# Gates of the PEER experts: high and low halves in one moving operand, one matmul per token

## The chip, the core and the metric

The kernel runs on one core of a Trainium2 chip. TensorE (PE, with its weight loads PEld) multiplies into PSUM banks of 512 float32 values on each of 128 partitions; VectorE (DVE) and ScalarE (ACT) work on SBUF and PSUM; SyncE (SP) issues the transfers. Each engine takes its own instructions in order. The metric is the time on the device in microseconds, median of several runs.

## The reference, cut to what matters

Two transformer blocks on 256 tokens of width 1024. The second has two layers, and each ends in a PEER stage: 16384 experts, of which every token uses 8 heads x 16.

```
def _peer(x, w_q, sub_keys, u, v):
    ...
    expert = idx_a * PEER_N_KEYS + idx_b          # first key a, second key b, 128 each
    gate = jax.nn.softmax(best_s, axis=-1)
    ...
        h = jnp.einsum('td,thkd->thk', xb, u[eb])
        a = (jax.nn.gelu(h, approximate=False) * gb).astype(xb.dtype)
        return jnp.einsum('thk,thkd->td', a, v[eb])
```

The kernel gathers nothing. It computes the hidden value of every expert for every token, multiplies it by a gate that is zero for experts not chosen, and multiplies the result by all of v.

## The kernel before

All matmuls with float32 data run as three passes over a high and a low part (`split`, L224: ScalarE writes `hi`, L225, VectorE writes `lo`, L226). In `peer`, `u_pair(j)` (L1225) loads two second keys' expert weights, splits them (four instructions of 128x1024), runs 48 matmuls of 256 columns (L264 to L266) and writes gelu into the ring `H` (L1228), which holds 80 second keys (`RING`) of 128 first keys by 256 tokens. `v_pair(j)` (L1271) splits two second keys of `H` (`ah`, `al`) and their weights and runs 24 matmuls of 512 columns (L281 to L283).

Between them stand the gates. The second keys are cut in parts of 48, 48 and 32 (`PARTS`), the tokens in groups of 16; so a layer has 48 calls of `gates(part, t0)` (L1230), and the kernel 96. One call does this. VectorE writes the one-hot rows `oa` (first key of each of a token's 128 choices, for 16 tokens) and `ob` (second key), then `oh` and `ol`, which are `ob` times the high and the low half of the gate (L1239 to L1242). The tokens lie innermost, four by four, so that the columns of one token stand 4 half-floats (8 bytes) apart. For each token TensorE multiplies `oa` by `oh` and by `ol` into the same columns of a PSUM bank (L1249, L1250); so the bank holds the sum. Banks of the tag `ms` are taken by eight tokens of 48 columns or sixteen of 32; there are two such banks. VectorE multiplies a full bank into `H` (L1257), in two instructions where the part wraps around the ring (the second part).

The loop at L1318 to L1335 emits the calls: the first part's 16 groups go with `u_pair` 24 to 39, which fills the ring; then u and v alternate; the second part's 16 groups go with u and v in turn, the third part's with v. A planner orders the instructions of each engine by their place in the program and by when their operands are ready in its own account, so matmuls of `u_pair` or `v_pair` can stand between those of one call. Preparation of weights runs 350 instructions ahead (`AHEAD`). `v_pair(0)` waits for all groups of the first part.

Of the kernel before, what the change touches and what calls it, by code (L numbers as in the profile page):

```python
# [9 lines left out]
F32 = mybir.dt.float32  # L10
F32R = mybir.dt.float32r
F16 = mybir.dt.float16
U32 = mybir.dt.uint32
AF = mybir.ActivationFunctionType
ALU = mybir.AluOpType
# [11 lines left out]
ALPHA = 4.0 ** 0.25  # L27
G_SCALE = 2048.0

PARTS = (48, 48, 32)  # second keys of the experts that are gated together  # L30
RING = 80  # second keys whose hidden values are on chip at a time
RATE = 0.96  # groups of 16 tokens gated for each tile of expert weights
AHEAD = 350  # instructions by which the weights' preparation runs ahead
WBUFS = 4  # split halves of weight tiles on chip
LEAD = 2  # tiles of the first block left when its attention is through
PACE = 2  # tiles of expert weights to a step of the selection
TURN = 17  # the tile after which the first half's indices are transposed
# memory keys and values of a layer, computed where norms leave the tensor engine free
FILL = ((), ("k1",), ("v1",), (), ("k0", "v0"))
URGENT = 1500  # instructions by which norms go before other work  # L40


def _btiles(w, cols):
# [128 lines left out]
class Net:  # L172
# [157 lines left out]
    def col(self, name="col", n=1, bufs=None):  # L330
        return self.sp.tile([128, n], F32, name=name, tag=f"{name}{n}")

    def table(self, func):
        """Has the table of func loaded behind the scalar engine's work so far."""
        t = self.col("warm")
        self.tc.keep_in_program_order(self.nc.scalar.activation(t, self.eps6, func))

# [56 lines left out]
    def layer_norm(self, acc, gb, xT=None, out=None):  # L394
# [3 lines left out]
        for tt in range(2):  # L398
# [14 lines left out]
            for nh in range(2):  # L413
# [6 lines left out]
                    nc.sync.dma_start(out[tt * 128:tt * 128 + 128, c], x[:, c])  # L420
                if xT is not None:
                    self.to_T(xT, x[:, c], tt, nk=4, k0=4 * nh)
# [1 line left out]
    def load_mem(self):  # L424
        self.memT = tuple(self.mp.tile([128, 8, S], F32R, name=f"memT{s}") for s in "hl")
        raw = self.raw(self.io["memT"].rearrange("p k t -> p (k t)")).rearrange("p (k t) -> p k t", k=8)
# [392 lines left out]
    def ple_gate(self, acc, bv, xT):  # L819
        nc = self.nc  # L820
        for tt in range(2):
            h = self.vp.tile([128, D], F32, name="hn", tag="hn")
            for nh in range(2):
# [3 lines left out]
                nc.vector.tensor_mul(h[:, c], h[:, c], self.pproj[:, tt, c])  # L827
                nc.vector.tensor_add(self.x[:, tt, c], self.x[:, tt, c], h[:, c])
                self.to_T(xT, self.x[:, tt, c], tt, nk=4, k0=4 * nh)
# [1 line left out]
    def mem_attn(self, qm, km, vm):  # L831
        nc, pp = self.nc, self.pp
        mP = {}
# [266 lines left out]
    def peer(self, l, xT):  # L1100
        nc, io, pp = self.nc, self.io, self.pp
# [5 lines left out]
        idx = [pp.tile([128, S], F16, name=f"pidx{j}") for j in range(4)]  # L1107
        H = pp.tile([128, RING, S], F32, name="H")
        tk = ExitStack()
# [120 lines left out]
        def gates(part, t0):  # L1230
            b0, nb = sum(PARTS[:part]), PARTS[part]
            oa = op.tile([128, 4, P_KEYS, 4], F16, name="oa", tag="oa", bufs=2)
            ob, oh, ol = (op.tile([128, 4, max(PARTS), 4], F16, name=n, tag=n, bufs=k)[:, :, :nb]
                          for n, k in (("ob", 1), ("oh", 2), ("ol", 2)))
            c = slice(t0, t0 + 16)
            col = lambda j, n: idx[j][:, c].rearrange("p (g t) -> p g t", t=4)[:, :, None, :].to_broadcast(
                [128, 4, n, 4])
            iot = lambda n0, n: iota[:, None, n0:n0 + n, :].to_broadcast([128, 4, n, 4])
            nc.vector.tensor_tensor(out=oa, in0=iot(0, P_KEYS), in1=col(0, P_KEYS), op=ALU.is_equal)  # L1239
            nc.vector.tensor_tensor(out=ob, in0=iot(b0, nb), in1=col(1, nb), op=ALU.is_equal)  # L1240
            nc.vector.tensor_tensor(out=oh, in0=ob, in1=col(2, nb), op=ALU.mult)
            nc.vector.tensor_tensor(out=ol, in0=ob, in1=col(3, nb), op=ALU.mult)  # L1242
            nt = 16 if nb <= 32 else 8
            for e in range(16 // nt):
                ps = self.ms()
                for n in range(nt):
                    t = e * nt + n
                    o = ps[:, n * nb:n * nb + nb]
                    nc.tensor.matmul(o, oa[:, t // 4, :, t % 4], oh[:, t // 4, :, t % 4], start=True, stop=False)  # L1249
                    nc.tensor.matmul(o, oa[:, t // 4, :, t % 4], ol[:, t // 4, :, t % 4], start=False, stop=True)  # L1250
                g = ps[:, :nt * nb].rearrange("p (t b) -> p b t", t=nt)
                done = 0
                while done < nb:
                    s = (b0 + done) % RING
                    n = min(nb - done, RING - s)
                    h = H[:, s:s + n, t0 + e * nt:t0 + e * nt + nt]
                    nc.vector.scalar_tensor_tensor(h, g[:, done:done + n], 1.0 / G_SCALE, h, op0=ALU.mult,  # L1257
                                                   op1=ALU.mult)
                    done += n

        acc = {}

# [36 lines left out]
        for tt in range(2):  # L1299
            todo += [lambda tt=tt: pick(tt, 0, 4), lambda tt=tt: pick(tt, 4, 4), lambda tt=tt: gate(tt),  # L1300
                     lambda tt=tt: lookup(tt)]
        n0 = PARTS[0] // 2
        for j in range(n0):
# [10 lines left out]
        op = ok.enter_context(self.tc.tile_pool(reuse_waits="tile", name="onehot", bufs=1))  # L1314
        ends = [sum(PARTS[:k + 1]) // 2 for k in range(len(PARTS))]
        queue = [(k, t0) for k in range(len(PARTS)) for t0 in range(0, S, 16)]
        up, vp, due, turn_v = n0, 0, 0.0, True
# [98 lines left out]
```

## Time and profile before

| what | value |
|---|---|
| median of 3 runs | 2532.6 us (2531.86 to 2533.39) |
| span of the profiled execution | 2531.2 us |
| PE / DVE / ACT busy in that span | 2497.7 / 1733.8 / 1194.2 us |
| gate matmuls (L1249, L1250) | 3072 |
| share of the chain that ended last, PE | 94% |

A "busy" TensorE has at least one matmul in flight; matmuls overlap, so what one costs is read from the distance of their starts. The page's chain of waits names for each stretch of time the engine that the end hung on.

### The profile page before, as it was taken

The page shows a single profiled execution, that of the slowest core. Times are in us where ns is not written, and L with a number is a line of the kernel's source. Part 1 is how long each engine was busy: PE and PEld are TensorE (multiplying, and loading weights), DVE is VectorE, ACT ScalarE, POOL GpSimd, SP SyncE. Part 2 cuts the span into 40 slices and gives each one's busy share as a digit, 9 for nine tenths or more (in the row PEclk, how much of TensorE's full clock was granted, in tenths as well). Part 3 has the DMA queues.
Part 4 walks back from the last instruction along what each step waited for, and adds up shares of the span by engine and source line. Part 5 has one row for each costly group of instructions (what it writes and reads, how often), then busy time and mean ns, then how long its engine had stood idle before and what let it go on. Part 6 is the DMA issues. An engine that isn't in the chain of part 4 may idle for free.

```text
span 2531.2 us, 44590 instructions
## 1 busy us (share of the span) xinstructions
PE 2497.7 (99%) x18560; PEld 2276.9 (90%) x18560; DVE 1733.8 (68%) x3195; ACT 1194.2 (47%) x1697; POOL 5.9 (0%) x17
## 2 busy tenths in 40 slices
PE   8999999999999999999999999999999999999998
PEld 7998899988799999999988888989999999998887
DVE  5357665565699587588478556669968758748756
ACT  5357554455545533433443445644643443344443
POOL 0000000000000000000000000000000000000000
PEclk9989999999999999999999999999999999999999
DMA  8422455543444544544544554344553454454454
GB/s 295 150 96 92 140 209 190 183 173 109 154 170 167 195 142 148 191 157 143 191 167 156 194 195 158 140 175 165 183 179 139 161 189 143 158 183 167 166 187 147
DMA packets 64410, 420.80 MB, mean 166 GB/s; under 512 B 7520, under 2 KB 10480, under 8 KB 15824
## 3 DMA queue, kind: packets, MB, share of 16 engines
q1 hardware_dynamic: 64208, 417.96, 47.4%
q8 instruction: 145, 2.38, 0.4%
q14 instruction: 57, 0.47, 0.1%
HBM read 416.88 MB, written 1.05 MB: 165 GB/s over the span
## 4 chain that ended last, share of the span: by engine, by line
PE 94%; DVE 3%; ACT 1%; DMA 1%; issue 1%; SPq 0%; DVEq 0%; ACTq 0%
PE ps_st L264 15%; PE ps_st L266 15%; PE ps_st L265 15%; PE ps_acc L281 12%; PE ps_acc L283 12%; PE ps_acc L282 12%; PE ps_ms L1249 3%; PE ps_ms L1250 3%; PE ps_sc L621 1%; PE ps_acc L640 1%; DVE lo L226 1%; ACT hi L225 1%; PE ps_acc L1152 1%; PE ps_sc L494 1%; PE ps_ms L1053 0%
## 5 line engine op out<-in xcount | busy, mean ns | idle before, releaser
L226 DVE TENSOR_TENSOR lo<-raw,hi 128x1024 fp32r<-128x1024 f32 (+1 forms) x762 | 922.8, 1214 | 508.5 <-ACT hi L225 505.5
L225 ACT CAST hi<-raw 128x1024 fp32r<-128x1024 f32 (+1 forms) x762 | 792.8, 1043 | 939.7 <-PE ps_st L265 610.1
L264 PE MATMUL ps_st<-xTh,hi 128*128 128x256 f32 (+1 forms) x3232 | 924.0, 286 | 0.9 <-DVE shift_v L573 0.7
L266 PE MATMUL ps_st<-xTh,lo 128*128 128x256 f32 (+1 forms) x3232 | 919.0, 284 | 0.5 <-DVE lo L226 0.5
L265 PE MATMUL ps_st<-xTl,hi 128*128 128x256 f32 (+1 forms) x3232 | 918.3, 284 | 0.0
L264 PEld LDWEIGHTS ps_st<-xTh,hi 128*128 128x128 f32 (+1 forms) x3232 | 619.3, 192 | 5.6 <-issue 2.0
L265 PEld LDWEIGHTS ps_st<-xTl,hi 128*128 128x128 f32 (+1 forms) x3232 | 618.8, 191 | 4.2 <-issue 1.4
L266 PEld LDWEIGHTS ps_st<-xTh,lo 128*128 128x128 f32 (+1 forms) x3232 | 618.4, 191 | 4.5 <-issue 2.7
L281 PE MATMUL ps_acc<-hi,ah 128*128 128x512 f32 x1024 | 403.8, 394 | 0.0
L282 PE MATMUL ps_acc<-lo,ah 128*128 128x512 f32 x1024 | 399.0, 390 | 0.0
L283 PE MATMUL ps_acc<-hi,al 128*128 128x512 f32 x1024 | 398.2, 390 | 0.0
L283 PEld LDWEIGHTS ps_acc<-hi,al 128*128 128x128 f32 x1024 | 192.1, 188 | 40.9
L281 PEld LDWEIGHTS ps_acc<-hi,ah 128*128 128x128 f32 x1024 | 192.9, 188 | 37.5
L282 PEld LDWEIGHTS ps_acc<-lo,ah 128*128 128x128 f32 x1024 | 192.6, 188 | 37.4
L225 ACT CAST ah<-H 128x512 fp32r<-128x512 f32 x128 | 79.5, 623 | 178.4 <-PE ps_acc L282 178.4
L226 DVE TENSOR_TENSOR al<-H,ah 128x512 fp32r<-128x512 f32 x128 | 88.4, 692 | 86.3 <-ACT ah L225 86.3
L1249 PE MATMUL ps_ms<-oh,oa 128*128 128x48 f16 (+1 forms) x1536 | 144.3, 214 | 0.0
L1249 PEld LDWEIGHTS <-oa 128*128 128x128 f16 x1536 | 131.1, 117 | 14.0 <-DVE lo L226 10.5
L1250 PE MATMUL ps_ms<-ol,oa 128*128 128x48 f16 (+1 forms) x1536 | 143.0, 214 | 0.0
L1250 PEld LDWEIGHTS <-oa 128*128 128x128 f16 x1536 | 133.9, 118 | 0.0
L1257 DVE SCALAR_TENSOR_TENSOR H<-ps_ms,H 128x256 f32<-128x256 f32 (+2 forms) x224 | 96.6, 457 | 40.7 <-PE ps_ms L1250 40.5
L1239 DVE TENSOR_TENSOR oa<-iota,pidx 128x2048 f16<-128x2048 f16 x96 | 116.7, 1215 | 0.0
(365 smaller groups left out, 2234.5 us busy)
## 6 DMA issues: line engine op xcount, KB each, us to landing
raw<-in_u SPq DMA_DIRECT2D x128, 1024.0 KB, 4.8
raw<-in_v SPq DMA_DIRECT2D x128, 1024.0 KB, 4.8
raw<-in_w_gu SPq DMA_DIRECT2D x22, 1024.0 KB, 4.8
raw<-in_w_pq SPq DMA_DIRECT2D x16, 1024.0 KB, 4.9
raw<-in_w_out SPq DMA_DIRECT2D x12, 1024.0 KB, 4.9
raw<-in_w_down SPq DMA_DIRECT2D x11, 1024.0 KB, 4.8
raw<-in_b_q SPq DMA_DIRECT2D x9, 1024.0 KB, 4.8
raw<-in_a_vr SPq DMA_DIRECT2D x6, 1024.0 KB, 4.9
```

Of the source, the lines that this page charges most:

```text
L225: self.nc.scalar.copy(hi, src)
L226: self.nc.vector.tensor_sub(lo, src, hi.bitcast(F32))
L264: mm(ps, wh, xh, start=first, stop=False)
L265: mm(ps, wh, xl, start=False, stop=False)
L266: mm(ps, wl, xh, start=False, stop=last)
L281: mm(ps, xh, w[0][:, c], start=first, stop=False)
L282: mm(ps, xh, w[1][:, c], start=False, stop=False)
L283: mm(ps, xl, w[0][:, c], start=False, stop=last)
L1239: nc.vector.tensor_tensor(out=oa, in0=iot(0, P_KEYS), in1=col(0, P_KEYS), op=ALU.is_equal)
L1249: nc.tensor.matmul(o, oa[:, t // 4, :, t % 4], oh[:, t // 4, :, t % 4], start=True, stop=False)
L1250: nc.tensor.matmul(o, oa[:, t // 4, :, t % 4], ol[:, t // 4, :, t % 4], start=False, stop=True)
L1257: nc.vector.scalar_tensor_tensor(h, g[:, done:done + n], 1.0 / G_SCALE, h, op0=ALU.mult, op1=ALU.mult)
```

## The change

`oh` and `ol` become one tile `og` that holds, for each four tokens, the columns of the high half and behind them those of the low half. One matmul per token and part multiplies `oa` by both, so 96 or 64 columns where two matmuls of 48 or 32 wrote into one place. High and low results lie side by side in PSUM, so a bank holds four tokens of 96 columns or eight of 64, half as many as before. ScalarE copies the high columns of a bank to an SBUF tile `gt`, VectorE adds the low ones, and when all 16 tokens are there VectorE multiplies `gt` into `H`. `gt` and `ob` have one buffer, `oa` and `og` two. The lines that only lose a comment are left out here.

```
-            ob, oh, ol = (op.tile([128, 4, max(PARTS), 4], F16, name=n, tag=n, bufs=k)[:, :, :nb]
-                          for n, k in (("ob", 1), ("oh", 2), ("ol", 2)))
+            ob = op.tile([128, 4, max(PARTS), 4], F16, name="ob", tag="ob")[:, :, :nb]
+            og = op.tile([128, 4 * 2 * max(PARTS) * 4], F16, name="og", tag="og", bufs=2)[:, :32 * nb].rearrange(
+                "p (g s b t) -> p g s b t", g=4, s=2, t=4)
+            gt = op.tile([128, max(PARTS) * 16], F32, name="gt", tag="gt")[:, :nb * 16].rearrange(
+                "p (b t) -> p b t", t=16)
...
-            nc.vector.tensor_tensor(out=oh, in0=ob, in1=col(2, nb), op=ALU.mult)
-            nc.vector.tensor_tensor(out=ol, in0=ob, in1=col(3, nb), op=ALU.mult)
-            nt = 16 if nb <= 32 else 8
+            for j in range(2):
+                nc.vector.tensor_tensor(out=og[:, :, j], in0=ob, in1=col(2 + j, nb), op=ALU.mult)
+            nt = 8 if nb <= 32 else 4
             for e in range(16 // nt):
                 ps = self.ms()
                 for n in range(nt):
                     t = e * nt + n
-                    o = ps[:, n * nb:n * nb + nb]
-                    nc.tensor.matmul(o, oa[:, t // 4, :, t % 4], oh[:, t // 4, :, t % 4], start=True, stop=False)
-                    nc.tensor.matmul(o, oa[:, t // 4, :, t % 4], ol[:, t // 4, :, t % 4], start=False, stop=True)
-                g = ps[:, :nt * nb].rearrange("p (t b) -> p b t", t=nt)
-                done = 0
-                while done < nb:
-                    s = (b0 + done) % RING
-                    n = min(nb - done, RING - s)
-                    h = H[:, s:s + n, t0 + e * nt:t0 + e * nt + nt]
-                    nc.vector.scalar_tensor_tensor(h, g[:, done:done + n], 1.0 / G_SCALE, h, op0=ALU.mult,
-                                                   op1=ALU.mult)
-                    done += n
+                    nc.tensor.matmul(ps[:, n * 2 * nb:(n + 1) * 2 * nb], oa[:, t // 4, :, t % 4],
+                                     og[:, t // 4, :, :, t % 4].rearrange("p s b -> p (s b)"), start=True, stop=True)
+                g = ps[:, :nt * 2 * nb].rearrange("p (t s b) -> p s b t", t=nt, s=2)
+                gs = gt[:, :, e * nt:e * nt + nt]
+                nc.scalar.copy(gs, g[:, 0])
+                nc.vector.tensor_tensor(out=gs, in0=gs, in1=g[:, 1], op=ALU.add)
+            done = 0
+            while done < nb:
+                s = (b0 + done) % RING
+                n = min(nb - done, RING - s)
+                h = H[:, s:s + n, t0:t0 + 16]
+                nc.vector.scalar_tensor_tensor(h, gt[:, done:done + n], 1.0 / G_SCALE, h, op0=ALU.mult, op1=ALU.mult)
+                done += n
```

## Rows read from the trace of the kernel before

**Rows 1.** Head of the page: span, and busy time of each engine.
```profile
span 2531.2 us, 44590 instructions
...
PE 2497.7 (99%) x18560; PEld 2276.9 (90%) x18560; DVE 1733.8 (68%) x3195; ACT 1194.2 (47%) x1697; POOL 5.9 (0%) x17
```

**Rows 2.** Busy time by stretch, layer 0: part one, part two, between, part three.
```profile
core 0: us, PE busy (x) PEld busy (x) DVE busy (x) ACT busy (x) POOL busy (x), PEclk, DMA share, GB/s
885.62:988.40 102.78, 102.78 (x1122) 102.21 (x1120) 82.86 (x112) 36.39 (x42) 0.00 (x0) 1.00 0.43 149
1096.12:1197.00 100.88, 100.88 (x954) 92.63 (x953) 88.77 (x148) 36.69 (x42) 0.00 (x0) 1.00 0.45 152
1197.00:1286.80 89.80, 89.80 (x578) 82.10 (x577) 45.11 (x41) 41.73 (x48) 0.00 (x0) 1.00 0.53 182
1300.00:1386.60 86.60, 86.60 (x730) 71.48 (x730) 73.55 (x99) 34.23 (x40) 0.00 (x0) 1.00 0.47 164
```

**Rows 3.** Groups by line and form: matmuls of the high half.
```profile
L1249 PE MATMUL ps_ms<-oh,oa 128*128 128x48 f16 x1024 | 105.8, 226 | 0.0
...
L1249 PE MATMUL ps_ms<-oh,oa 128*128 128x32 f16 x512 | 38.5, 191 | 0.0
```

**Rows 4.** Timeline of PE (start, duration), a group of part one.
```profile
885.38 0.28 PE L265 MATMUL ps_st<-xTl,hi 128*128 128x256 f32 x1
885.50 0.28 PE L266 MATMUL ps_st<-xTh,lo 128*128 128x256 f32 x1
885.62 0.21 PE L1249 MATMUL ps_ms<-oh,oa 128*128 128x48 f16 x1
...
887.14 0.36 PE L264 MATMUL ps_st<-xTh,hi 128*128 128x256 f32 x1
887.34 0.28 PE L265 MATMUL ps_st<-xTl,hi 128*128 128x256 f32 x1
```

**Rows 5.** Timeline of PE, a group of part three.
```profile
1299.99 0.20 PE L1249 MATMUL ps_ms<-oh,oa 128*128 128x32 f16 x1
...
1301.08 0.47 PE L281 MATMUL ps_acc<-hi,ah 128*128 128x512 f32 x1
1301.39 0.39 PE L282 MATMUL ps_acc<-lo,ah 128*128 128x512 f32 x1
1301.62 0.40 PE L283 MATMUL ps_acc<-hi,al 128*128 128x512 f32 x1
```

**Rows 6.** Timeline of DVE, within one step of part one.
```profile
908.62 0.56 DVE L1257 SCALAR_TENSOR_TENSOR H<-ps_ms,H 128x384 f32<-128x384 f32 x1 [0.98 <-PE ps_ms L1250]
909.10 1.22 DVE L226 TENSOR_TENSOR lo<-raw,hi 128x1024 fp32r<-128x1024 f32 x1
```

**Rows 7.** Busy time of one step in parts one, two (two groups) and three.
```profile
892.97:900.31 7.34, 7.34 (x83) 7.30 (x81) 5.92 (x8) 2.59 (x3) 0.00 (x0) 1.00 0.42 145
1124.97:1139.38 14.41, 14.41 (x139) 13.23 (x137) 12.82 (x21) 5.25 (x6) 0.00 (x0) 1.00 0.43 143
1320.00:1326.60 6.60, 6.60 (x57) 5.46 (x56) 5.79 (x9) 2.58 (x4) 0.00 (x0) 1.00 0.44 156
```

**Rows 8.** Groups by line and form: prices of VectorE.
```profile
L1257 DVE SCALAR_TENSOR_TENSOR H<-ps_ms,H 128x384 f32<-128x384 f32 x64 | 35.3, 554 | 30.8 <-PE ps_ms L1250 30.6
...
L1257 DVE SCALAR_TENSOR_TENSOR H<-ps_ms,H 128x256 f32<-128x256 f32 x64 | 26.8, 419 | 9.9 <-PE ps_ms L1250 9.9
...
L1257 DVE SCALAR_TENSOR_TENSOR H<-ps_ms,H 128x512 f32<-128x512 f32 x32 | 21.9, 691 | 0.0
...
L226 DVE TENSOR_TENSOR lo<-raw,hi 128x768 fp32r<-128x768 f32 x16 | 14.9, 949 | 5.7 <-ACT hi L225 5.7
...
L655 DVE TENSOR_TENSOR os<-ps_acc,wsw 128x384 f32<-128x384 f32 x16 | 8.9, 557 | 16.6 <-PE ps_acc L644 16.6
```

**Rows 9.** Groups by line and form: copies of ScalarE out of PSUM.
```profile
L637 ACT COPY PT<-ps_pt 128x512 f32<-128x512 f32 x16 | 9.1, 584 | 2.5 <-PE ps_pt L634 2.5
...
L637 ACT COPY PT<-ps_pt 128x256 f32<-128x256 f32 x16 | 6.0, 372 | 4.3 <-PE ps_pt L634 4.2
```

## The prediction, made blind

> **What bounds the kernel now.** I read the head of the page first: TensorE is busy for 2497.7 of 2531.2 us, VectorE for 68%, ScalarE for 47% [rows 1]. [...] Then the matmuls themselves, by the distance of their starts in the timeline, and the prices of the added work.
>
> **TensorE, gate matmuls.** There are 1024 pairs of 48 columns and 512 of 32 [rows 3], each with as many matmuls of the low half as of the high. A group of 16 tokens issues 32 matmuls. With 48 columns it runs from 885.62 to 887.14: 1.52 us, 47.5 ns a matmul. Behind it the first 256-column matmul takes 0.20 us to the next start, where 0.12 is usual: 0.08 us for leaving the gates [rows 4]. So 1.60 us a group. With 32 columns it is 1299.99 to 1301.08, 34 ns a matmul, and the 512-column matmul behind takes 0.31 instead of 0.23: 1.09 + 0.08 = 1.17 us [rows 5].
>
> What does a matmul of 96 or 64 columns cost? No row shows it with this operand, whose columns lie 8 bytes apart. From 32 to 48 columns the price rises by 13.5 ns, 0.84 ns a column, and 34 = 32 x 0.84 + 7. On that line a matmul of 64 costs 61 ns and one of 96 costs 88; the pair costs 68 and 95. So joining two saves just the 7 ns that do not depend on columns. The other end is the slope of packed operands: from 256 to 512 columns 0.12 to 0.23 us, 0.43 ns a column [rows 4, 5], which gives 47.5 + 48 x 0.43 = 68 and 34 + 32 x 0.43 = 48 ns. I take the first end, since its slope is from this very operand and 47.5 ns for 48 columns is more than twice what 0.43 allows.
>
> [...]
>
> **Bursts.** A group's 16 tokens now need four fillings of the two `ms` banks in parts one and two, where two were enough. The third filling waits until ScalarE has copied and VectorE has added the first. The planner will put u or v matmuls there, and each return to them costs up to the 0.08 us above, or less: the last gate matmul is now longer by 41 ns and can hide that much of the next weights' arrival, so 0.04 to 0.08. With one burst a group costs 16 x 88 ns + 0.04 = 1.45 us; with four at 0.08 it costs 1.73. I take two bursts at 0.06: 1.53 us, 0.07 less than now. 64 groups: 4.5 us gained (bounds: 9.6 gained, 8.3 lost). Part three fits its two banks: 16 x 61 + 80 ns = 1.06 us, 0.11 less; 32 groups: 3.5 us gained. TensorE in all: 8 us gained.
>
> **VectorE.** A step is bounded by starts, and an instruction blocks the next for about 0.08 us less than its duration (0.56 long, next start 0.48 later) [rows 6]. A plain two-operand instruction costs what the fused one costs (557 and 554 for 384 values) [rows 8], so an add of 192 values, on the line through 256 and 384 (1.05 ns a value), takes 0.35 us, or 0.27 blocked. `og` costs what `oh` and `ol` cost: same values, same instructions.
> - Part one, a step of 7.34 us with 5.92 busy [rows 7]: less two of 554 (0.95 blocked), plus four adds (1.08) and one multiply of 768 values (949, so 0.87): 6.92.
> - Part two, two groups in 14.41 us with 12.82 busy [rows 7]: each group loses two of 256 and two of 128 values (419 and, on the same line, 284 ns: 1.09 blocked), gains four adds (1.08), one of 512 (0.61) and one of 256 (0.34): 12.82 + 1.9 = 14.7. That is more than the step. The backlog, 0.3 us x 8 steps, can run into the next stretch, where VectorE is half idle and nothing needs the second part yet.
> - Part three, 6.60 us with 5.79 busy [rows 7]: two adds of 256 (0.34 each) more: 6.47.
>
> So no step is over, or its excess has a place to go, but the reserve falls from 1.4 us to 0.4 in part one and to nothing in the others, and VectorE's in-order queue now waits for ScalarE four times a group. Bounds of these waits: nothing (today TensorE does not stop in any of these stretches with VectorE at 88% [rows 2]), or today's idle time kept on top in part one: 6.92 + 1.42 = 8.34 us for a step of 7.27, 1.07 x 32 steps = 34 us. I take 4 us, nearer to nothing, because that idle time is mostly time in which VectorE has nothing due (0.98 us ahead of one L1257 [rows 6]).
>
> **ScalarE** gets four copies of 192 values (line through 256 and 512, 0.83 ns a value: 0.32 us) or two of 256 (0.37) [rows 9]: 1.3 us on 2.59 of 7.34 busy [rows 7]. That is hidden; its price shows only as the bank's later return. Loads, queues and SP's work are untouched.
>
> **Sum.** 2531.2 - 8 + 4 = 2527.2 us of span; the runs' median stands 1.4 us above the span, so 2528.6; I say 2529.
>
> **Rivals.**
> 1. The columns cost the packed slope: 68 and 48 ns. A group costs 16 x 68 + 2 x 0.06 = 1.21 (0.39 less, 64 times: 25 us) and 16 x 48 + 80 ns = 0.85 (0.32 less, 32 times: 10 us). VectorE then limits part one (6.92 of 6.95) and part two, so some 10 us stay behind: 2532.6 - 25 = 2507. For it: the first gate matmul of a burst lasts as long with 32 columns as with 48 (0.20 and 0.21) [rows 4, 5]. Against it: the steady slope. Chance 0.14.
> 2. VectorE becomes the bound. Place: the 32 steps of part one, whose last group `v_pair(0)` waits for. Price: the 34 us above, of which the planner hides perhaps a third: 2529 + 22 = 2551. It decides once VectorE's waits in a step exceed 7.27 - 6.92 = 0.35 us. For it: four hand-overs from ScalarE where none was, behind casts that themselves wait for TensorE. Against: preparation runs ahead by 350 instructions. Chance 0.17.
> 3. TensorE stops for the bank: the third filling's turn comes before the first is added. A turn is a matmul (0.22), a copy (0.32) and an add (0.35), 0.9 us, of which the second filling covers 0.35; 0.5 us x 64 groups = 32, less the 8: 2556 if the planner puts nothing between, 2540 if it covers two thirds. It decides when ScalarE's cast of 128x1024 stands ahead of a copy. Chance 0.13.
> 4. TensorE's best: one burst, no waits, 2532.6 - 13 = 2519 to 2527. Chance 0.19.
>
> **How the numbers follow.** The forecast, 2529 with its own range 2527.5 to 2537.7, has 0.37, and with the bursts and waits uncertain it is no change that can be told: a measurement of this kernel can tell about 0.2%, 5 us. Faster by more: rivals 1 and 4, 0.33. Slower: 2 and 3, 0.30. The range goes from rival 1 to rival 2, 2506 to 2552, and leaves out a third rival without cover and a first rival without give-back, under 2 in 10.
>
> **What would show it.** Starts of gate matmuls 88 and 61 ns apart: the column price; 68 and 48: rival 1. Runs of 8 gate matmuls split by L264 to L266: the bursts. Idle PE ahead of gate matmuls, ended by the add: rival 3; idle PE ahead of L264 or L281, ended by `lo`, `ah` or `al`: rival 2. VectorE's busy share in part one should be 94 to 97%. The forecast is wrong if the slope per column changes beyond 48, or if TensorE shows idle time in the stretches that have none now.

## The result, and the profile after

The changed kernel takes 2553.5 us (median of 4 runs, 2551.4 to 2556.1) where the kernel before takes 2532.4 in the same session: a ratio of 1.0084, 95% interval 1.0070 to 1.0097. It is slower by 21 us; my range ended at 2552. The profiled execution has a span of 2553.4 us, 22.2 more than before [rows 1].

The head of its page:

```profile
span 2553.4 us, 42136 instructions
...
PE 2499.9 (98%) x17024; PEld 2265.0 (89%) x17024; DVE 1814.2 (71%) x3419; ACT 1275.3 (50%) x2017; POOL 5.9 (0%) x17
```

TensorE's busy time is 2.2 us more than before, so most of what was lost is time in which it has nothing in flight. Busy time by stretch says where (columns as in [rows 2]): layer 0, the steps of part one, their end, and two stretches behind that.

```profile
885.00:990.00 105.00, 105.00 (x923) 103.06 (x922) 92.91 (x145) 51.45 (x99) 0.00 (x0) 1.00 0.43 148
993.10:1005.90 12.80, 4.47 (x42) 3.54 (x41) 12.25 (x23) 4.13 (x11) 0.00 (x0) 0.65 0.23 83
1005.90:1010.60 4.70, 4.70 (x11) 3.73 (x12) 4.21 (x9) 1.50 (x4) 0.00 (x0) 0.50 0.01 3
1012.00:1016.00 4.00, 4.00 (x20) 3.28 (x19) 2.62 (x3) 1.78 (x3) 0.00 (x0) 1.00 0.00 0
```

In the steps TensorE never stops, and VectorE is busy for 88% of them. Then comes a stretch of 12.8 us in which TensorE works for 4.5 and VectorE for 12.3. Inside it the granted clock falls to 0.50, where it stays behind it for a while: 11 matmuls take 4.7 us, where behind that 20 take 4.0. TensorE's timeline of that end (start, duration, idle time before and what ended it):

```profile
992.86 0.28 PE L266 MATMUL ps_st<-xTh,lo 128*128 128x256 f32 x1
996.30 0.89 PE L1251 MATMUL ps_ms<-og,oa 128*128 128x96 f16 x8 [3.17 <-DVE og L1245]
997.75 0.89 PE L1251 MATMUL ps_ms<-og,oa 128*128 128x96 f16 x8 [0.56 <-DVE gt L1256]
999.07 0.89 PE L1251 MATMUL ps_ms<-og,oa 128*128 128x96 f16 x8 [0.43 <-DVE gt L1256]
1002.23 0.88 PE L1251 MATMUL ps_ms<-og,oa 128*128 128x96 f16 x8 [2.28 <-DVE gt L1256]
1004.38 0.89 PE L1251 MATMUL ps_ms<-og,oa 128*128 128x96 f16 x8 [1.27 <-DVE og L1245]
1005.90 0.79 PE L281 MATMUL ps_acc<-hi,ah 128*128 128x512 f32 x1 [0.63 <-ACT ah L225]
```

The last u matmul ahead of the stop starts at 992.86. It belongs to `u_pair(40)`, which the planner has pulled ahead of `v_pair(0)`: the gelu of `u_pair(39)` starts at 986.80. `v_pair(0)` may start when the first part's last group is in `H`, and 40 gate matmuls, two and a half groups, are still to come, with nothing to lay between them. Each eight wait for `og` or for the add that gives a bank back, and `v_pair(0)` for its cast `ah`: 8.3 us idle. Layer 1 has the same rows from 2007 on.

Work of more than two groups is left when the cover ends, although in the steps VectorE stands idle for 12.1 of 105 us, most of it behind ScalarE in the order of its queue (waits of VectorE, 885 to 990: us in total, times, longest):

```profile
DVE gt L1256 <- ACT gt L1255: 5.0, 10, 1.0
DVE lo L226 <- ACT hi L225: 4.0, 6, 1.7
DVE oa L1242 <- PE ps_ms L1251: 1.9, 3, 0.8
```

What is left it does in the stretch behind, where it is busy for 12.3 us and TensorE waits. A second, smaller stop stands in part three:

```profile
1392.58 1.77 PE L283 MATMUL ps_acc<-hi,al 128*128 128x512 f32 x4 [1.52 <-DVE al L226]
```

The gate matmuls, two returns to u matmuls, and the prices of the added work (groups by line and form):

```profile
892.52 0.89 PE L1251 MATMUL ps_ms<-og,oa 128*128 128x96 f16 x8
893.19 0.36 PE L264 MATMUL ps_st<-xTh,hi 128*128 128x256 f32 x1
893.39 0.28 PE L265 MATMUL ps_st<-xTl,hi 128*128 128x256 f32 x1
...
895.90 0.53 PE L1251 MATMUL ps_ms<-og,oa 128*128 128x96 f16 x4
896.20 0.36 PE L265 MATMUL ps_st<-xTl,hi 128*128 128x256 f32 x1
896.41 0.52 PE L1251 MATMUL ps_ms<-og,oa 128*128 128x96 f16 x4
```
```profile
L1256 DVE TENSOR_TENSOR gt<-gt,ps_ms 128x192 f32<-128x192 f32 x256 | 81.3, 350 | 13.3 <-ACT gt L1255 12.8
...
L1255 ACT COPY gt<-ps_ms 128x192 f32<-128x192 f32 x256 | 72.2, 319 | 67.7 <-PE ps_ms L1251 37.4 <-DVE H L1262 24.0 <-DVE ob L1243 5.5
...
L1262 DVE SCALAR_TENSOR_TENSOR H<-gt,H 128x768 f32<-128x768 f32 x32 | 30.5, 954 | 0.0
```

By the distance of their starts (median over all of a form) a matmul of 96 columns costs 90 ns and one of 64 costs 62. A group has mostly three bursts, of 8, 4 and 4. In the rows eight matmuls lead to the next start after 0.67 us, 0.05 under 8 x 90, and that next matmul takes 0.20 instead of 0.12; over all 160 returns from 96 columns to a u matmul the median of this sum is 0.04 us a burst, not 0.08.

**The balance.** Idle time: 8.3 + 1.5 us a layer, 19.7. The profile counts idle time only from the end of the matmul before, so each of the 14 stops takes 0.16 to 0.18 us more from the distance of starts: 2.5. Half clock: v matmuls that start at granted 0.50 stand further apart than at 1.00 (0.43 instead of 0.23 us), together by 2.3 and 1.45 us in layer 0 and 2.0 and 1.5 in layer 1, 7.3; the gate matmuls there keep their 90 ns. That is 29.4; the span grew by 22.2, so matmuls and bursts gave 7.2.

### The profile page after: what moved, and what is told of

Read it like the earlier page. It is cut to its first block, busy times and chain, and to the rows that moved or that the text cites. A ratio compares the mean times of both kernels' runs of the same rounds, so it can differ in the third digit from the quotient of the medians.

```text
span 2553.4 us, 42136 instructions
## 1 busy us (share of the span) xinstructions
PE 2499.9 (98%) x17024; PEld 2265.0 (89%) x17024; DVE 1814.2 (71%) x3419; ACT 1275.3 (50%) x2017; POOL 5.9 (0%) x17
## 4 chain that ended last, share of the span: by engine, by line
PE 92%; DVE 4%; ACT 2%; DMA 1%; issue 1%; SPq 0%; DVEq 0%; ACTq 0%
PE ps_st L264 15%; PE ps_st L265 15%; PE ps_st L266 15%; PE ps_acc L281 12%; PE ps_acc L283 12%; PE ps_acc L282 11%; PE ps_ms L1251 5%; DVE lo L226 1%; PE ps_sc L621 1%; PE ps_acc L640 1%; ACT hi L225 1%; PE ps_acc L1152 1%; PE ps_sc L494 1%; PE ps_ms L1053 0%; PE ps_pt L634 0%
## 5 line engine op out<-in xcount | busy, mean ns | idle before, releaser
L226 DVE TENSOR_TENSOR lo<-raw,hi 128x1024 fp32r<-128x1024 f32 (+1 forms) x762 | 924.0, 1215 | 475.8 <-ACT hi L225 472.3
L282 PE MATMUL ps_acc<-lo,ah 128*128 128x512 f32 x1024 | 405.0, 395 | 0.0
L283 PE MATMUL ps_acc<-hi,al 128*128 128x512 f32 x1024 | 400.8, 394 | 3.0 <-DVE al L226 3.0
L283 PEld LDWEIGHTS ps_acc<-hi,al 128*128 128x128 f32 x1024 | 194.0, 190 | 43.4 <-DVE al L226 4.1
L1251 PE MATMUL ps_ms<-og,oa 128*128 128x96 f16 (+1 forms) x1536 | 163.6, 258 | 15.5 <-DVE og L1245 8.9
L1251 PEld LDWEIGHTS <-oa 128*128 128x128 f16 x1536 | 109.9, 119 | 41.6 <-issue 17.1
L1255 ACT COPY gt<-ps_ms 128x192 f32<-128x192 f32 (+1 forms) x320 | 93.7, 330 | 72.1 <-PE ps_ms L1251 40.1
L1256 DVE TENSOR_TENSOR gt<-gt,ps_ms 128x192 f32<-128x192 f32 (+1 forms) x320 | 105.4, 363 | 13.6 <-ACT gt L1255 12.8
L281 PE MATMUL ps_acc<-hi,xTh 128*128 128x512 f32 (+1 forms) x272 | 108.3, 398 | 5.2 <-ACT xTh L225 3.3
```

The costliest lines, as they stand in the source:

```text
L226: self.nc.vector.tensor_sub(lo, src, hi.bitcast(F32))
L281: mm(ps, xh, w[0][:, c], start=first, stop=False)
L282: mm(ps, xh, w[1][:, c], start=False, stop=False)
L283: mm(ps, xl, w[0][:, c], start=False, stop=last)
L1251: nc.tensor.matmul(ps[:, n * 2 * nb:(n + 1) * 2 * nb], oa[:, t // 4, :, t % 4], og[:, t // 4, :, :, t % 4].rearrange("p s b -> p (s b)"), ...
L1255: nc.scalar.copy(gs, g[:, 0])
```

## The experiments

Times are medians; the kernel before had 2531.9 to 2533.1 in these sessions. A ratio is to it, with its 95% interval.

### Is it the wait for a bank? (e1)

On the changed kernel, every second filling of part one goes to the `acc` banks, which `v_pair` does not hold yet:

```
-                ps = self.ms()
+                ps = self.acc() if part == 0 and e % 2 else self.ms()
```

> The changed kernel, in which every second filling of a group of the first part takes one of the four acc banks that v_pair has not yet claimed, so that a group's four fillings have four banks. Theory A (VectorE's added work of about 1 us a group makes it fall behind in the first part; what is left at its end is worked off with TensorE idle, and the idle time costs the clock): still some 8 us idle a layer behind u_pair 39, 2550 to 2556 us. Theory B (the way fill, copy, add, bank free is too slow for two banks): with four banks the idle time falls under 3 us a layer, 2522 to 2535 us.

Measured: 2562.9 us, 1.0117 (1.0088 to 1.0146), above the range of either theory. Idle time at the end of part one is 6.9 us a layer, most of what it was, now ended by `og` (4.1) and `ah` (2.8) and no more by a bank, and a new stop of 4.4 us stands ahead of an L283 at 1215, ended by `al`. More banks don't cure it, so the return of a bank is where TensorE happens to stand, not why it is late.

### Matmuls alone, hand-over alone, load alone (e3 to e7, e11)

e3 has the joined matmuls but no copies and adds: VectorE multiplies the high half straight into `H` and leaves the low half out.

```
-                nc.scalar.copy(gs, g[:, 0])
-                nc.vector.tensor_tensor(out=gs, in0=gs, in1=g[:, 1], op=ALU.add)
...
+                    h = H[:, s:s + n, t0 + e * nt:t0 + e * nt + nt]
+                    nc.vector.scalar_tensor_tensor(h, g[:, 0, done:done + n], 1.0 / G_SCALE, h, op0=ALU.mult,
+                                                   op1=ALU.mult)
```

> The changed kernel without its sum: VectorE multiplies the high half straight from PSUM into H, four instructions of 192 values a group; the low half is computed and not used, ScalarE's copies and VectorE's adds are left out. It holds the matmuls of the change alone. Theories A and B: no idle time at the end of the first part, and the whole gain of TensorE shows, 7 us a layer: 2514 to 2522 us. If it stays above 2528, the matmuls themselves do not gain.

Measured: 2525.5 us, 0.9964 (0.9948 to 0.9980), no idle TensorE in any gate stretch; the time is above the 2514 to 2522 expected, which counted the gain once for each layer. The head of its page:

```profile
span 2524.0 us, 41718 instructions
...
PE 2489.4 (99%) x17024; PEld 2257.5 (89%) x17024; DVE 1749.9 (69%) x3419; ACT 1193.6 (47%) x1697; POOL 5.9 (0%) x17
```

So joining gives 7 us where VectorE's work is not in the way (span 7.2 under the kernel before), as the balance says (7.2), with all its bursts.

e4 keeps the old pairs and lets ScalarE copy each bank and VectorE multiply once a group. e5 keeps the old pairs and gives each group an add on VectorE that nobody needs (896 values, in part three 576). e7 has both. The first line is e4's, the others are e5's (e7 writes its add as half-floats, which takes as long: 1084 and 1083 ns):

```
+                nc.scalar.copy(gt[:, :, e * nt:e * nt + nt], g)
...
+            scr = op.tile([128, 896], F32, name="scr", tag="scr")[:, :w]
+            nc.vector.tensor_add(scr, self.x[:, 0, :w], self.x[:, 1, :w])
```

> The kernel before, with its pairs of matmuls, but each full bank is copied to SBUF by ScalarE and VectorE multiplies the 16 tokens from there: hand-over to ScalarE without more work for VectorE (one multiply of 768 in place of two of 384). Theory A: as the kernel before, 2529 to 2536 us, no idle TensorE behind u_pair 39. Theory B: idle time of 4 to 8 us a layer there, 2542 to 2555 us.

> The kernel before with one more VectorE instruction a group that nobody waits for: an add of 896 values (576 in the third part), about 1.0 and 0.7 us, the work that the change adds to VectorE, without hand-overs. Theory A: VectorE falls behind, TensorE is idle for 4 to 9 us a layer behind u_pair 39 and loses clock, 2545 to 2562 us. Theory B: as the kernel before, 2529 to 2536 us.

> The kernel before with ScalarE's copy of each full bank to SBUF, one multiply by VectorE from there, and one more VectorE add a group that nobody waits for (896 values, 576 in the third part): load and hand-over together on the old pairs of matmuls, whose step is 7.34 us. Theory A (the shorter step is needed too): 2529 to 2537 us, no idle TensorE behind u_pair 39. Theory B (load and hand-over together make the lag): idle time of 4 to 9 us a layer there, 2542 to 2558 us.

Measured: 2532.8, 1.0004 (0.9993 to 1.0015); 2532.2, 0.9999 (0.9987 to 1.0010); 2532.1, 1.0006 (0.9994 to 1.0017). None has idle TensorE in a gate stretch. e7's stretch of part one:

```profile
885.00:990.00 105.00, 105.00 (x1159) 104.36 (x1158) 98.63 (x116) 47.86 (x72) 0.00 (x0) 1.00 0.43 147
```

VectorE is busier there (94%) than in the changed kernel (88%), and it costs nothing. So VectorE's share doesn't decide.

e6 is e3 with the idle add (768 or 512 values): joined matmuls, load, no hand-over. e11 is the changed kernel with `oa` computed once a part instead of once a group (the other groups' first keys are left out): joined matmuls, hand-over, less load. The first line is e6's, the others are e11's:

```
+            nc.vector.tensor_add(scr, self.x[:, 0, :w], self.x[:, 1, :w])
...
-            nc.vector.tensor_tensor(out=oa, in0=iot(0, P_KEYS), in1=col(0, P_KEYS), op=ALU.is_equal)
+            if t0 == 0:
+                nc.vector.tensor_tensor(out=oa, in0=iot(0, P_KEYS), in1=col(0, P_KEYS), op=ALU.is_equal)
```

> The kernel of the high half alone (matmuls of the change, four multiplies of 192 straight from PSUM, neither copies nor adds; the low half is not used), with one more VectorE instruction a group that nobody waits for, an add of 768 values (512 in the third part): VectorE's load of the change on TensorE's steps of the change, without ScalarE in between. Theory A (load against the shorter step: VectorE's need of 6.9 us plus its usual waits no longer fits a step of 7.1 us): idle TensorE of 4 to 9 us a layer behind u_pair 39, 2535 to 2555 us. Theory B (the load hurts only where it stands in the way from a filled bank to a free one, by way of ScalarE): as without the extra add, 2521 to 2529 us.

> The changed kernel with oa computed only for the first 16 tokens of each part and used for all its groups, so that gates of the other tokens stand at wrong first keys: it takes 1.13 us a group from VectorE and leaves copies, adds, banks and matmuls as they are. Theory A (VectorE's load against TensorE's shorter step): no idle TensorE behind u_pair 39 and no lost clock, 2514 to 2524 us. Theory B (the chain from bank to bank by way of ScalarE): still some 8 us idle a layer, 2545 to 2556 us.

Measured: e6 2540.2, 1.0030 (1.0019 to 1.0042), theory A's; e11 2538.7, 1.0030 (1.0019 to 1.0041), between its two theories. Both stop at the end of part one; TensorE's timelines there, e6 and then e11:

```profile
996.86 0.89 PE L1252 MATMUL ps_ms<-og,oa 128*128 128x96 f16 x8 [1.01 <-DVE og L1243]
999.26 0.88 PE L1252 MATMUL ps_ms<-og,oa 128*128 128x96 f16 x8 [1.51 <-DVE H L1260]
1001.84 0.79 PE L281 MATMUL ps_acc<-hi,ah 128*128 128x512 f32 x1 [1.70 <-ACT ah L225]
```
```profile
994.58 0.89 PE L1256 MATMUL ps_ms<-og,oa 128*128 128x96 f16 x8 [2.54 <-DVE gt L1261]
995.91 0.52 PE L1256 MATMUL ps_ms<-og,oa 128*128 128x96 f16 x4 [0.44 <-DVE gt L1261]
996.64 0.52 PE L1256 MATMUL ps_ms<-og,oa 128*128 128x96 f16 x4 [0.21 <-DVE gt L1261]
998.63 0.79 PE L281 MATMUL ps_acc<-hi,ah 128*128 128x512 f32 x1 [1.47 <-ACT ah L225]
```

On the joined matmuls the two causes add up, as far as medians of runs that spread over 3 to 6 us can tell: neither (e3) 2525.5, load 14.7 more, hand-over 13.2 more, both (the changed kernel) 28.0 more. In e11 VectorE is busy for 84.5 of the 105 us (before: 83.6), so there the chain from matmul to copy, add and multiply makes the stop by itself.

### How late the groups are

The stop is read best from one distance: the end of a group's last multiply behind the start of the gelu of the u pair it was emitted with, group 1 with `u_pair(24)` to group 16 with `u_pair(39)`. Four rows give the last group's, the first two of the kernel before, the others of the changed one (timelines of ACT and DVE):

```profile
989.47 0.60 ACT L1228 ACTIVATE H<-ps_st 128x512 f32<-128x512 f32 x1
...
993.25 0.56 DVE L1257 SCALAR_TENSOR_TENSOR H<-ps_ms,H 128x384 f32<-128x384 f32 x1
```
```profile
986.80 0.59 ACT L1228 ACTIVATE H<-ps_st 128x512 f32<-128x512 f32 x1
...
1004.24 0.95 DVE L1262 SCALAR_TENSOR_TENSOR H<-gt,H 128x768 f32<-128x768 f32 x1
```

That is 4.3 us before (993.81 - 989.47) and 18.4 after. All groups of layer 0, in us:

| kernel | group 1 | groups 2 to 15 | group 16 | idle TensorE at the end of part one |
|---|---|---|---|---|
| before | 7.9 | 9.4 | 4.3 | 0 |
| e5 old pairs, load | 8.1 | 9.4 to 9.8 | 5.4 | 0 |
| e4 old pairs, hand-over | 9.1 | 10.7 | 8.3 | 0 |
| e7 old pairs, load, hand-over | 8.1 | 9.7 to 10.7 | 4.7 | 0 |
| e18 old pairs, four fillings | 7.7 | 9.4 | 5.9 | 0 |
| e3 joined, neither | 7.7 | 9.2 | 6.8 | 0 |
| e13 old pairs, four fillings, load | 8.9 | 9.4 to 11.0 | 8.2 | 1.5 |
| e6 joined, load | 8.9 | 9.2 to 13.7 | 11.7 | 4.2 |
| e11 joined, hand-over | 12.4 | 13.9 to 14.1 | 13.0 | 4.7 |
| e16 changed, groups earlier | 7.5 | 5.4 to 17.6 | 13.9 | 6.3 |
| e1 changed, more banks | 12.3 | 11.0 to 16.7 | 15.7 | 6.9 |
| changed | 13.1 | 12.4 to 22.0 | 18.4 | 8.3 |
| e15 changed, tokens two by two | 12.5 | 11.2 to 20.4 | 17.5 | 8.7 |

On the joined matmuls the hand-over makes every group some 5 us later from the first on (e11 against e3; on the old pairs, e4, it is 1.3). The load lets the lag grow from group to group (e6), and in the changed kernel both do. While u matmuls are left the lag costs nothing; at the end of part one most of what exceeds some 7 us of it is idle time. About that much cover is left when the gelu of `u_pair(39)` starts: in the changed kernel the u matmuls of `u_pair(40)` last from there to 992.86, 6.1 us. In e4 a lag of 8.3 costs nothing, since 32 gate matmuls of part two stand there as well (996.44 to 997.90).

### Four fillings or a shorter step? (e13, e18)

On the old pairs neither load nor hand-over cost anything. The joined matmuls differ in two things: TensorE's step is shorter, and a group has four fillings. Both runs are the kernel before with half-filled banks; e13 has the idle add, the last line, as well.

```
-            nt = 16 if nb <= 32 else 8
+            nt = 8 if nb <= 32 else 4
...
+            nc.vector.tensor_add(scr, self.x[:, 0, :w], self.x[:, 1, :w])
```

> Old pairs of matmuls, nothing copied or added, but banks only half filled, so a group has four fillings instead of two and twice as many multiplies of half the size; and each group gets an independent VectorE add of 768 or 512 values, as large as the load of the change. TensorE's step stays 7.3 us or a little over, so VectorE keeps its slack. Theory A (the joined matmuls shorten TensorE's step, and that uses up the slack): no idle TensorE, 2530 to 2538. Theory F (it is the four fillings a group, each with its own start on VectorE): TensorE idle 4 us a layer or more at the end of part one, as with the joined matmuls and the same load, 2538 to 2552.

> Old pairs of matmuls and half-filled banks, four fillings a group (two in the third part), with no added load: the run e13 without its independent add. If the fillings alone cost what e13 measured (more returns to gate matmuls, each 0.08 us, and the tail): 2542 to 2549. If fillings and load are needed together: 2532 to 2537, all of it returns (some 20 to 40 more a layer, 2 to 3 us each layer at most).

Measured: e13 2547.4, 1.0057 (1.0040 to 1.0074); e18 2541.6, 1.0036 (1.0022 to 1.0050). e13's time is that of theory F, but its idle time is only a third of what F wanted. e18 has no idle TensorE in a gate stretch, and its time is at the edge of its first case: on the old pairs the fillings alone cost 9 us. No engine's wait accounts for them; in TensorE's starts they are the returns from more bursts, 0.08 us each behind a last matmul of 47 ns (in the changed kernel it was 0.04 behind one of 90): 172 in parts one and two where the kernel before has 68, and 8.8 us more in all. The load on top costs 6 us, with 1.5 us idle a layer and a half clock of 3.4 us in one layer. So four fillings and the load together start the stop without a shorter step, but only to a third of e6's; what the rest of e6's lag comes from is not settled. Four fillings with the hand-over were not run on the old pairs.

### The price of a column (e9, e10, e12, e14, e15)

e9, e10 and e12 put a token's columns side by side in memory. In e9 GpSimd writes `oh` and `ol` so; in e10 ScalarE repacks them for parts one and two; in e12 it repacks `og` of the changed kernel. One line of each, in this order:

```
+                nc.gpsimd.tensor_tensor(out=o.rearrange("p g t b -> p g b t"), in0=ob, in1=col(2 + j, nb), op=ALU.mult)
...
+                    nc.scalar.copy(mv[-1].rearrange("p g t b -> p g b t"), o)
...
+                nc.scalar.copy(mv[:, :, :, j].rearrange("p g t b -> p g b t"), og[:, :, j])
```

> The kernel before with its pairs of matmuls, but oh and ol are written by GpSimd, so that a token's columns lie side by side: measures what the 8-byte spacing of the columns costs TensorE, and takes two instructions a group from VectorE. If the spacing makes the column price of 0.84 ns: starts of 48-column matmuls come down from 47 to 33 to 37 ns, 20 to 29 us less in all, 2503 to 2514 us as long as two GpSimd instructions stay under 7 us a group. If the column price has another cause: 47 ns as before and 2530 to 2536 us.

> The kernel before with its pairs of matmuls; in the parts of 48 columns ScalarE copies oh and ol so that a token's columns lie side by side. VectorE's work stays as it was, ScalarE gets two copies of 768 half-floats a group. The column price by the spacing: starts 34 ns apart instead of 47, 13 ns x 2048 = 27 us less, if VectorE follows the shorter step (5.9 us of need, 0.4 of waits, a step of 6.9): 2503 to 2512 us. If the copies come too late for TensorE, 2520 us or more, with TensorE idle ahead of the gate matmuls.

> The changed kernel in which ScalarE also repacks both halves, so that the 96 or 64 columns of a token lie side by side (ob is built inside og to find room for it). The price of a joined matmul with packed columns: some 50 ns for 96, 35 for 64. Theory A: the step gets shorter by another 0.6 us, VectorE's load is the same, so the idle time behind u_pair 39 grows and eats it: 2545 to 2565 us, no faster than the change as it was. If the gain of the matmuls comes through, 2520 us or less.

Measured: 2755.8, 1.0884 (1.0850 to 1.0917); 2680.0, 1.0583 (1.0566 to 1.0601); 3011.3, 1.1891 (1.1867 to 1.1915). All three are far slower, and the groups say why: the first two of e9, the third of e10.

```profile
L1243 POOL TENSOR_TENSOR oh<-ob,pidx 128x768 f16<-128x768 f16 x64 | 292.3, 4568 | 1325.8 <-DVE ob L1241 1165.9 <-PE ps_ms L1251 157.6 <-PE ps_st L265 2.3
...
L1240 DVE TENSOR_TENSOR oa<-iota,pidx 128x2048 f16<-128x2048 f16 x96 | 234.3, 2441 | 3.5 <-PE ps_ms L1251 3.5
```
```profile
L1247 ACT COPY ohp<-oh 128x768 f16<-128x768 f16 x64 | 243.3, 3801 | 8.0 <-DVE oh L1241 8.0
```

One such write takes ScalarE 3.8 us and GpSimd 4.6, and VectorE's `oa` takes 2441 ns on average beside GpSimd instead of 1215. As measurements they serve. With packed columns gate matmuls of 48 columns start 33 ns apart at granted 1.00 instead of 47, and those of 32 as before, 33 (e9, e10); in e12 64 packed columns also start 33 ns apart, and 96 start 43. So in these runs 33 ns is a floor, the same for 32, 48 and 64 columns, and above it the price goes with the distance of the columns (96 of them: 90 ns at 8 bytes, 43 side by side).

e14 leaves all on VectorE and moves the tokens only, two by two instead of four by four, so that columns stand 4 bytes apart, in `oa` too. e15 does the same to the changed kernel.

```
-            oa = op.tile([128, 4, P_KEYS, 4], F16, name="oa", tag="oa", bufs=2)
+            oa = op.tile([128, 8, P_KEYS, 2], F16, name="oa", tag="oa", bufs=2)
...
-                    nc.tensor.matmul(o, oa[:, t // 4, :, t % 4], oh[:, t // 4, :, t % 4], start=True, stop=False)
+                    nc.tensor.matmul(o, oa[:, t // 2, :, t % 2], oh[:, t // 2, :, t % 2], start=True, stop=False)
```

> The kernel before with the tokens innermost two by two instead of four by four, in oa, ob, oh and ol: a token's columns lie 4 bytes apart, not 8. VectorE's instructions keep their number of values. If the distance of the columns sets TensorE's price and 4 bytes are near enough: gate matmuls of 48 columns start 34 ns apart instead of 47, 13 ns times 2048 = 27 us less, minus what VectorE can't follow: 2503 to 2514. If 4 bytes cost what 8 do: 2530 to 2534. If VectorE's instructions get dearer with the shorter inner run (2 values instead of 4): oa above 1215 ns and idle TensorE, above 2536.

> The changed kernel with the two-by-two layout of the tokens. If 4 bytes give TensorE the price of packed columns: 96 columns start some 50 ns apart instead of 90, so TensorE's step in part one shortens to 6.5 us, below what VectorE needs with copies and adds (6.9): theory A expects more idle TensorE than in the changed kernel, and a time of 2535 to 2565, not the 41 us less that the matmuls alone would give. If idle time stays what it is (8 us a layer): 2515 or less. If 4 bytes cost what 8 do: 2553.

Measured: e14 2478.8 us (2476.3 to 2480.7), 0.9788 (0.9772 to 0.9804); e15 2502.3, 0.9880 (0.9860 to 0.9900). e14 beats both kernels, and gains twice what was expected. Its gate matmuls (first and last of 30 in a row), and the groups of its weight loads and of `oa`:

```profile
888.82 0.18 PE L1249 MATMUL ps_ms<-oh,oa 128*128 128x48 f16 x1
...
889.55 0.18 PE L1250 MATMUL ps_ms<-ol,oa 128*128 128x48 f16 x1
```
```profile
L1239 DVE TENSOR_TENSOR oa<-iota,pidx 128x2048 f16<-128x2048 f16 x96 | 116.7, 1215 | 0.0
L1250 PEld LDWEIGHTS <-oa 128*128 128x128 f16 x1536 | 82.0, 97 | 0.0
```

0.73 us over 29 steps is 25 ns, and with 32 columns it is 25 as well: now the floor itself has come down from 33, and the weight load, whose columns also moved together, lasts 97 ns (before: 118). No run moved the weights' columns alone. VectorE's instructions cost what they did (`oa` 1215 ns). The sum fits: 22 ns x 2048 + 8.5 ns x 1024 = 54 us, measured 54.3.

In e15 the joined matmuls start 44 and 30 ns apart. TensorE's step in part one (mean distance of the gelus of `u_pair` 24 to 39) is 6.59 us instead of 7.08, with the same order of every instruction on TensorE, VectorE and ScalarE as in the changed kernel. Its end of part one, three rows of six:

```profile
985.64 0.52 PE L1251 MATMUL ps_ms<-og,oa 128*128 128x96 f16 x8 [3.10 <-DVE og L1245]
...
988.22 0.88 PE L1251 MATMUL ps_ms<-og,oa 128*128 128x96 f16 x8 [0.39 <-DVE gt L1256]
991.42 0.80 PE L1251 MATMUL ps_ms<-og,oa 128*128 128x96 f16 x8 [2.32 <-DVE gt L1256]
```

The idle time is the changed kernel's almost row by row (8.7 and 8.3 us), though fifteen steps are 7 us shorter and VectorE is busy for 91.6 of 95 us (885 to 980). That is the second case of its expectation, and theory A falls: a lag made by a lack of VectorE time would have grown with the shorter step. It did not, which speaks for the written order: where the 40 last gate matmuls stand, and behind what on VectorE's queue. That is argued from one order at two speeds; e16 and e17 below change the order. Against e14 the change costs 23.5 us on the faster layout too, about what it costs on the slower one.

### Can the stop be moved away? (e8, e16, e17, e19)

e8 has parts of 40, 48 and 40 second keys on the changed kernel.

```
-PARTS = (48, 48, 32)
+PARTS = (40, 48, 40)
```

> The changed kernel with parts of 40, 48 and 40 second keys in place of 48, 48 and 32: the 16 groups of the first part go with 20 u_pairs instead of 16, so VectorE has a quarter more time for each. Both theories: VectorE keeps up, no idle TensorE and no lost clock at the end of the first part, 2518 to 2532 us; the third part has 40 columns now, four fillings a group. If some 8 us a layer stay idle, it is not a lag that builds up over the first part.

Measured: 2570.0, 1.0150 (1.0120 to 1.0181), far above the 2518 to 2532 expected. The stop at the end of part one is gone, but one of 3.6 us now stands at the end of part two (1172), and three of 2.3 us in part three (1355, 1388 and 1420), whose 40 keys need four fillings instead of two. Since two things moved, it decides little.

e16 and e17 emit the first part's groups about one u pair earlier, on the changed kernel and on e15.

```
-RATE = 0.96
+RATE = 1.02
```

> The changed kernel with RATE 1.02 instead of 0.96: the same instructions, but the groups of the first part are emitted about one u_pair earlier. In the written order of TensorE, 20 gate matmuls then stand together ahead of v_pair(0), where the changed kernel has 40 (the kernel before has 16, with u matmuls around them). Theory O (VectorE's work for the last groups is behind in the written order, and those 40 have nothing beside them): idle TensorE at the end of part one falls from 8.3 us a layer to 3 to 5, the half clock behind it to 7 to 10 us, and the time to 2533 to 2544. Theory V (VectorE can't do the work of part one in the time of the 16 steps): the backlog is the same, idle TensorE stays 8 us or turns up ahead of L264, and the time stays at 2548 to 2556.

> The changed kernel with the two-by-two layout of the tokens and RATE 1.02. The written order is that of the run with RATE 1.02 and the four-by-four layout; TensorE's step in part one is shorter by 0.5 us, and VectorE's instructions are the same. Theory O: idle time falls by the same 3 to 5 us a layer as there, so 2502 - 10 to 20: 2482 to 2492. Theory V: VectorE, 97% busy in part one of the two-by-two layout at RATE 0.96, has no room for the earlier work, idle TensorE stays at 8 us a layer or more, 2498 or above.

Measured: e16 2567.2, 1.0142 (1.0125 to 1.0159); e17 2517.3, 0.9940 (0.9923 to 0.9956): slower by 14 and 15 us than the changed kernel and e15, from which they are made. Both theories missed e16's total; e17's is theory V's. TensorE's timeline of e16, end of part one and of part two (the third row has two of the four gate matmuls that stand there):

```profile
996.52 0.89 PE L1251 MATMUL ps_ms<-og,oa 128*128 128x96 f16 x8 [3.21 <-DVE og L1245]
997.91 0.88 PE L1251 MATMUL ps_ms<-og,oa 128*128 128x96 f16 x8 [0.51 <-DVE gt L1256]
1001.39 0.35 PE L1251 MATMUL ps_ms<-og,oa 128*128 128x96 f16 x2 [2.60 <-DVE og L1245]
...
1186.69 0.89 PE L1251 MATMUL ps_ms<-og,oa 128*128 128x96 f16 x8 [5.83 <-DVE og L1245]
```

The first stop shrinks only from 8.3 to 6.3 us, since the lag, 5.4 us for the second group, grows to 13.9 again; and part two, whose groups are earlier now too, gets a stop of 5.8 us that it did not have. So an earlier emission doesn't pay for the growing lag, and the stop at the end of part two stands where the prediction saw VectorE's need exceed the step and took it for harmless.

e19 has the two-by-two layout, old pairs in parts one and two, and the change in part three alone.

```
+            if nb > 32:
...
+                    ps = self.ms()
...
+                        nc.tensor.matmul(o, oa[:, t // 2, :, t % 2], og[:, t // 2, 0, :, t % 2], start=True, stop=False)
+                        nc.tensor.matmul(o, oa[:, t // 2, :, t % 2], og[:, t // 2, 1, :, t % 2], start=False, stop=True)
...
+                return
```

> Tokens two by two everywhere; the first two parts keep the old pairs and their two fillings, the third part alone has the joined matmuls, copies and adds. Against the two-by-two kernel (2478.8): 512 pairs of 50 ns become one matmul of 30 ns, 10 us less, if VectorE follows; its need in a step of the third part is 6.47 us of blocked time by the prediction's working, and TensorE's step there becomes 5.9. If the loss sits at the end of the first part alone: 2468 to 2474. If the third part's VectorE work costs as it does in the run with all three parts joined (idle 1.7 us a layer ahead of L283 and half clock behind it): 2474 to 2480.

Measured: 2476.9 (2473.4 to 2477.5), 0.9780 (0.9764 to 0.9797): not told apart from e14. The matmuls' 10 us are mostly taken back by a stop of 1.7 to 2.0 us a layer ahead of an L283, ended by `al`, and a half clock of 3.4 us behind one of them.

## Why the prediction was wrong, step by step

- **The column price was right in size, for a partly wrong reason.** Forecast 88 and 61 ns, measured 90 and 62. But the line went through two rows of which one, 32 columns at 34 ns, stands on the 33 ns floor that the packed runs showed. At 8 bytes 48, 64 and 96 columns cost 0.94 to 0.98 ns a column (47, 62 and 90 ns), and 32 cost 33 to 34; at 4 bytes 96 columns cost 44 ns (e15), side by side 43 (e12). Rival 1 stands refuted for this layout: no row has 68 or 48.
- **Bursts.** Taken as two of 0.06 us; there were three of 0.04. Number and price were off in opposite ways, so that their product came out by luck. Matmuls and bursts gave 7 us (balance and e3 7.2) where 8 was forecast.
- **Prices on VectorE and ScalarE** were right: add 350 ns (0.35), copy 319 (0.32), multiply 954 (949).
- **"I take 4 us" for the waits is the step that failed.** Measured were 19.7 us of idle TensorE, inside the bounds of 0 and 34, but not where the term was looked for. It was worked out per step, need against step (6.92 of 7.27), and in the steps TensorE never stopped; VectorE was busy 88% there, not 94 to 97: it stood waiting in its queue while the groups were late. The idle time stands after the last step, where 40 gate matmuls have no u matmul beside them and the chain og, matmul, copy, add, multiply lies bare. The prediction asked whether VectorE can follow, not how late it is when the cover ends.
- **Half clock stood nowhere in the sum.** The 12.8 us with 4.5 of work, and the 1.5 us stop in part three, are each followed by a granted clock of 0.50, which cost 7.3 us more. With the idle time and the edges of the stops (2.5) this is 29.4 us against a gain of 7.2.
- **Rival 2 named the place** (the last group of part one, for which `v_pair(0)` waits) and nearly the time, 2551. Its turning point, waits of 0.35 us in a step, is not what decided: e7 has VectorE fuller and costs nothing, e11 has it as empty as before and costs 13 us more than e3. That its time came out near is luck: its price was waits in 32 steps, and in the steps TensorE had none.
- **Rival 3's rows appear** (idle time ahead of gate matmuls, ended by the add), but only at the end of a part and for 3.3 of the 8.3 us; 4.4 are ended by `og`, which no rival had named, and more banks (e1) did not help.
- **Part two** was judged rightly: its excess ran into the next stretch (last multiply at 1232 us, before at 1193) without a stop. With the groups emitted earlier (e16) there was one, of 5.8 us.

What stays open: why the load lets the lag grow on the joined matmuls and not on the old pairs with two fillings. e15 speaks for the written order, but e16 and e17, whose order is another, missed what that theory forecast; which of the planner's costs writes the order so was not tried.

## What to carry to other kernels

Where an engine covers another's latency, look at the last pieces of a phase for themselves: read how far the last result lags behind the last covering matmul, and count what a longer chain adds to that, whatever the mean load says. Idle TensorE can cost twice, once as idle time and again at the lower clock behind it: both stops of the changed kernel did (19.7 us idle, then 7.3 us lost at granted 0.50), e16's stops of 1.5 us in part three did not. Before joining matmuls to save a fixed price, measure what the distance of their operands' columns costs: moving the tokens from four by four to two by two gave 54 us without a single instruction more.

## What the hardware showed that I had not expected

- At 8 bytes between columns the price of 96 columns does not follow TensorE's clock: they start 90 ns apart at granted 1.00 and at 0.50 (medians of 752 and 62 starts in the changed kernel). At 4 bytes (e15) it is 44 and 80 ns. So at 8 bytes something other than that clock sets their price; what it is was not shown.
- The floor of a gate matmul is not one number: 33 ns with `oa` at 8 bytes, even with the moving columns side by side (e9, e10, e12), and 25 with both operands at 4 (e14), whether the moving operand has 48 columns or 32. That the weights make the difference was not shown.
- Writing 128x768 half-floats so that neighbours in time land 96 bytes apart took ScalarE 3801 to 4093 ns (e10) and GpSimd 4427 to 4568 (e9), while VectorE's instruction on `oa` beside GpSimd took 2441 ns instead of 1215.
